# x^T from the host, the first norm folded into q, k, v and gate, transposed out-projections, in a two-layer decoder trunk

## The chip, the cores and the metric

The kernel runs on one core of one Trainium2 chip. The metric is device time in microseconds of one execution. Engines: PE (TensorE, matmuls and transposes), DVE (VectorE), ACT (ScalarE), POOL (GpSimd), SP (SyncE, here the queue that issues all DMAs).

## What is computed

x is 1024 x 1024 (1024 positions, model width 1024), float32. Layer A is differential attention with 8 heads, layer B stick-breaking attention with 16 heads of width 64, worked on in 8 pairs; both have a SiLU gate:

```python
h = rms(x, a_norm)                       # rms: x * rsqrt(mean(x*x) + 1e-6) * gain
q, k, v, g = split(h @ a_w_in)           # 1024 columns each
q, k = rope(rms(q, q_norm)), rope(rms(k, k_norm))     # norm over 64 columns
o = rms((softmax(q1 k1) - lam * softmax(q2 k2)) v, subln) * (1 - lambda_init)
x1 = x + (o * silu(g)) @ a_w_out
k, v = split(rms(x1, kv_norm) @ w_kv)
q, g = split(rms(x1, b_norm) @ b_w_in)
out = x1 + (stick_breaking(q, k, v) * silu(g)) @ b_w_out
```

All products keep more than one float32r matmul's precision: each operand is split into a high part h (rounded to float32r) and a low part l = value - h, and a product is three matmuls, h*h + h*l + l*h.

## The kernel before

Positions are worked on in two halves of 512 and blocks of 128; kc counts the 8 chunks of 128 of the model width. The normed input of a layer lies transposed as the pair (ah, al), [128 of a chunk, 8 chunks, 512 positions] for each half. Layer A's head h needs four projections: q and k together by rows (`qk_steps`, line 624: 8 row blocks, 256-wide matmuls with ah stationary and the weights moving), v and gate transposed (`proj_t`, line 233: 512-wide with the weights stationary). Layer B's k, v, q and gate all go through `proj_t`. `group` (line 211) writes the matmuls of one sum into a PSUM bank of the tag "proj" (2 banks) and cuts them into steps; `merge` (line 313) interleaves the steps of the next head's projections with the attention of the current one (`unit_s`, `unit_t`). `Jobs` loads the weights one job ahead. For the last head the fill is the out-projection.

`norm_rows` (line 125) norms one block of 128 positions: square with a row sum on ACT, `rstd_of` (line 112: Ln and Exp on ACT, one Newton step on DVE), scaling on DVE, 8 transposes by PE into PSUM, then h by ACT and l by DVE. It is called for the 8 blocks of x at the start (lines 718 to 729) and by `sink_a` (line 763) for the 8 blocks of x1. The gains of the norms are multiplied into the weights when these are split (`split_w` with gain, lines 158 to 165; `park`, line 178, which splits layer B's weights during layer A and writes them back to DRAM).

`OutProj` has the mixer output oT stationary (`lhs`, line 449) and the out-weights moving, 256 columns at a time (`parts`, line 452; c counts four column groups), or 512 for the last two chunks of the first two groups (`rest`, line 465). A sum is added into a tile of 128 positions x 1024 (`xs`, lines 457 and 469) that held the residual. `sink_a` or `sink_b` follows when a block has its last column group. The half f0 is projected beside the last head's second half, f1 after it: `pre1` takes the first six chunks of one or two column groups ahead, lines 543 and 544 the rest in the order 2, 3, 1, 0.

`v_rows` (line 303) evacuates v from PSUM by ACT, then transposes it back to rows; `silu` (line 237) evacuates the gate by DVE with a clamp at -80, and has Exp, Ln, Exp on ACT and a product on POOL, set late.

The order of instructions on each engine is fixed when the kernel is built: a planner takes the code's order as priority, moves `hp()` blocks ahead and `later()` blocks back, and places instructions by estimated durations; on the chip each engine runs its own queue strictly in that order. Tiles of one tag share a number of buffers (B, line 45), and a tile that finds none free waits.

## Time and profile before

| | us |
|---|---|
| median of three runs | 1450.12 |
| lowest, highest | 1446.09, 1452.68 |
| profiled execution | 1446.61 |
| its span, first to last instruction | 1444.8 |
| busy: PE, DVE, ACT, POOL | 1400.6, 1052.9, 907.9, 299.7 |

Times within the profile count from the start of the span. An engine's busy time is the time in which at least one of its instructions ran; matmuls overlap in the pipeline, so the length of one is more than its share of PE. PEclk is the granted TensorE clock as a share of full speed.

### The profile page before, as it was taken

Reading aid. Unit: us, or ns where it says so; the run is one execution under the profiler, and the core shown is the slowest. Engines: PE = TensorE matmul, PEld = TensorE weight load, DVE = VectorE, ACT = ScalarE, POOL = GpSimd, SP = SyncE. Lnnn points to the kernel's source line nnn. Section 1 sums busy time; section 2 is a strip of 40 time slices with the busy share of each in tenths; the row PEclk is TensorE's granted clock in tenths of the full one; section 3 lists DMA queues with packets and bytes.
Section 4 is the critical chain, followed back from the end, with each engine's and each line's share of the span. In section 5 each row is a group of like instructions: output and inputs, shape, how many; then the busy total and the mean of one; then the engine's idle time right before and its main releaser. Section 6 shows DMA issues by size and latency. Waiting matters only on the chain. (4 is left out here: it accounts for less than half of the span.)

```text
span 1444.8 us, 24738 instructions
## 1 busy us (share of the span) xinstructions
PE 1400.6 (97%) x8944; PEld 1179.3 (82%) x8944; DVE 1052.9 (73%) x2145; ACT 907.9 (63%) x1834; POOL 299.7 (21%) x545
## 2 busy tenths in 40 slices
PE   8999999999999999989999999999999999988899
PEld 8887878787878787879987777787788778777699
DVE  7577888787879787885514867787868777878851
ACT  7566766676767565544225776778777777777610
POOL 0111212121212113000001231322324132424200
PEclk9999999999999999999999999999999999998999
DMA  5246453645464645641522121131212121343524
GB/s 205 82 152 193 145 194 122 200 135 190 132 199 145 219 154 184 203 176 74 171 83 88 59 73 53 52 114 43 78 59 89 58 88 59 136 157 126 224 89 145
DMA packets 94603, 185.93 MB, mean 129 GB/s; under 512 B 8721, under 2 KB 43793, under 8 KB 93457
## 3 DMA queue, kind: packets, MB, share of 16 engines
q1 hardware_dynamic: 94480, 184.35, 38.1%
q8 instruction: 71, 1.16, 0.3%
q14 instruction: 52, 0.42, 0.1%
HBM read 119.31 MB, written 65.01 MB: 128 GB/s over the span
## 5 line engine op out<-in xcount | busy, mean ns | idle before, releaser
L223 PE MATMUL proj<-ah,w 128*128 128x512 f32 x768 | 309.2, 403 | 0.0
L225 PE MATMUL proj<-ah,w 128*128 128x512 f32 x768 | 308.9, 402 | 0.0
L224 PE MATMUL proj<-al,w 128*128 128x512 f32 x768 | 307.5, 400 | 0.0
L223 PE MATMUL proj<-w,ah 128*128 128x256 f32 x992 | 285.8, 288 | 6.6 <-DVE v L457 3.9
L224 PE MATMUL proj<-w,ah 128*128 128x256 f32 x992 | 281.8, 284 | 0.0
L225 PE MATMUL proj<-w,al 128*128 128x256 f32 x992 | 280.9, 283 | 0.0
L223 PEld LDWEIGHTS proj<-w,ah 128*128 128x128 f32 x992 | 187.7, 189 | 15.3 <-DVE v L457 4.9
L224 PEld LDWEIGHTS proj<-w,ah 128*128 128x128 f32 x992 | 187.7, 189 | 5.1 <-issue 4.5
L225 PEld LDWEIGHTS proj<-w,al 128*128 128x128 f32 x992 | 187.7, 189 | 1.7 <-issue 0.6
L225 PEld LDWEIGHTS proj<-ah,w 128*128 128x128 f32 x768 | 144.3, 188 | 37.6 <-issue 7.1
L223 PEld LDWEIGHTS proj<-ah,w 128*128 128x128 f32 x768 | 144.3, 188 | 36.8 <-issue 6.3
L224 PEld LDWEIGHTS proj<-al,w 128*128 128x128 f32 x768 | 144.4, 188 | 34.9 <-issue 5.1
L855 DVE TENSOR_TENSOR_SCAN u4k<-zl,u4k 128x768 f32<-128x768 f32 (+4 forms) x96 | 171.4, 1791 | 1.1
L300 DVE TENSOR_TENSOR tl<-tr,th 128x512 fp32r<-128x512 f32 (+1 forms) x240 | 145.1, 628 | 33.7 <-ACT th L299 33.0
L265 PE MATMUL sc<-kh,q 64*128 64x512 f32 (+2 forms) x768 | 156.6, 396 | 10.7 <-DVE small L655 7.5
L856 ACT ACTIVATE zl<-u4k 128x768 f32<-128x768 f32 (+4 forms) x96 | 81.4, 848 | 112.9 <-DVE u4k L855 98.8
L299 ACT ACTIVATE th<-tr 128x512 fp32r<-128x512 f32 (+1 forms) x240 | 125.2, 552 | 30.7 <-PE tr L293 22.5
L853 DVE SCALAR_TENSOR_TENSOR u4k<-zl,u4k 128x768 f32<-128x768 f32 (+4 forms) x96 | 95.9, 1008 | 58.5 <-ACT u4k L852 58.1
L843 POOL TENSOR_SCALAR_AFFINE_SELECT zl<-zl 128x128 f32<-128x128 f32 (+1 forms) x96 | 80.3, 845 | 278.3 <-ACT zl L841 278.1
L293 PE MATMUL tr<-ident,zl 128*128 128x128 f32 x864 | 130.7, 279 | 5.0 <-DVE tl L300 3.0
L265 PEld LDWEIGHTS sc<-kh,q 64*128 64x128 f32 x768 | 75.3, 185 | 58.7 <-issue 19.9
L664 ACT ACTIVATE zl<-zl,small 128x256 f32<-128x256 f32 (+7 forms) x128 | 98.1, 767 | 34.6 <-DVE small L655 18.7
(150 smaller groups left out, 2581.5 us busy)
## 6 DMA issues: line engine op xcount, KB each, us to landing
w<-w_kv SPq DMA_DIRECT2D x32, 512.0 KB, 5.2
w<-w_b SPq DMA_DIRECT2D x32, 512.0 KB, 5.2
w<-w_o SPq DMA_DIRECT2D x24, 512.0 KB, 4.7
raw<-in_w_kv_dram SPq DMA_DIRECT2D x32, 256.0 KB, 2.9
w_kv<-ph SPq DMA_DIRECT2D x32, 256.0 KB, 2.8
w_kv<-raw SPq DMA_DIRECT2D x32, 256.0 KB, 3.2
raw<-in_w_b_dram SPq DMA_DIRECT2D x32, 256.0 KB, 3.0
w_b<-ph SPq DMA_DIRECT2D x32, 256.0 KB, 3.0
```

Of the source, the lines that this page charges most:

```text
L223: pe.matmul(box["p"], lh, rh, start=(j == 0), stop=False)
L224: pe.matmul(box["p"], lh, rl, start=False, stop=False)
L225: pe.matmul(box["p"], ll, rh, start=False, stop=last)
L265: pe.matmul(pts[:, c, :wm], q[a][HI[c], rs_], k[b][HI[c], off:off + wm], start=(a + b == 0), stop=(a == 1))
L293: pe.transpose(pt[:, o:o + P], a[:, (2 * t + b) * P:(2 * t + b + 1) * P], ident)
L299: act.activation(th[:, skip:], pt[:, skip:], AF.Copy)
L300: dve.tensor_tensor(tl[:, skip:], pt[:, skip:], f32(th[:, skip:]), ALU.subtract)
L664: act.activation(p[c][:, :n], p[c][:, :n], AF.Exp, bias=b, scale=-1.0, accum_out=s[:, c:c + 1])
L843: pool.affine_select(t3[:, :, n - P:], t3[:, :, n - P:], [[0, len(cs)], [-1, P]], ALU.is_ge, -BIG, base=-1, channel_multiplier=1)
L853: dve.scalar_tensor_tensor(u, zc, 0.0, u, ALU.min, ALU.subtract)
L855: dve.tensor_tensor_scan(ur, t[:, 1:w2 + 1][:, ::-1], ur, 0.0, ALU.add, ALU.subtract)
L856: act.activation(zc, u, AF.Exp, scale=-1.0)
```

## The change

x comes from the host as x^T in 8 chunks, [8, 128, 1024], x1 is kept in the same form, and the output leaves transposed (the host turns it back). The first norm: with r the factor 1/rms of a position, x^T times the gain is split into (ah, al) without r. For q and k the factor cancels in their own norm, if its epsilon is divided by r squared (`eps_r`); v and gate, which come transposed, are multiplied by `rx`, r along the free axis in all partitions, when they leave PSUM. r comes from squares on ACT, added up on POOL over the chunks, and `rstd_cols`: one-column matmuls add over the partitions, `rstd_of` follows, then four diagonal matrices and four matmuls with ones bring r to all partitions. Both out-projections have the weights stationary and oT moving, 512 wide; the residual tiles hold two chunks x 512 positions, and a sum goes to the sink when its last chunk is added. `sink_a` collects the squares of a half's 8 pieces, and after the eighth calls `rstd_cols` and scales and splits all 8. The gains leave `split_w`. The clamp of layer A's gate moves to POOL, v's evacuation in layer A from ACT to DVE. The buffers change: g2k 2 in layer A, raw 4 instead of 3 (with `park`'s high parts, which had the tag ph with 2), small 8 instead of 9.

```diff
-    g2k = lambda: T("g2k", [P, HALF], B["g2k"])
+    g2k = lambda: T("g2k", [P, HALF], B["g2k" + "ab"[layer[1]]], pool=layer[0])
...
-    def rstd_of(ss, n, scale):
-        ln = small(n)
-        act.activation(ln, ss, AF.Ln, bias=eps, scale=scale)
+    def rstd_of(ss, n, scale, eps_r=None):
+        m = small(n)
+        if eps_r is None:
+            dve.tensor_scalar(m, ss, scale, EPS, ALU.mult, ALU.add)
+        else:
+            j = n // eps_r.shape[1]
+            dve.scalar_tensor_tensor(m.rearrange("p (k j) -> p k j", j=j), ss.rearrange("p (k j) -> p k j", j=j), scale,
+                                     eps_r.unsqueeze(2).to_broadcast([P, n // j, j]), ALU.mult, ALU.add)
         y = small(n)
...
+        act.activation(y, m, AF.Ln)
+        act.activation(y, y, AF.Exp, scale=-0.5)
...
-    def norm_rows(x, ah, al, r):
-        xn = zt()
-        ss = small(1)
-        act.activation(xn, x, AF.Square, accum_out=ss)
-        y = rstd_of(ss, 1, 1.0 / D)
-        dve.tensor_scalar(xn, x, y, None, ALU.mult)
-        for g in range(2):
-            t = PS("tr", B["tr"])
-            for j in range(4):
-                kc = g * 4 + j
-                pe.transpose(t[:, j * P:(j + 1) * P], xn[:, kc * P:(kc + 1) * P], ident)
-            t3 = t.rearrange("p (k c) -> p k c", k=4)
-            h = ah[:, g * 4:g * 4 + 4, r * P:(r + 1) * P]
-            l = al[:, g * 4:g * 4 + 4, r * P:(r + 1) * P]
-            act.activation(h, t3, AF.Copy)
-            dve.tensor_tensor(l, t3, f32(h), ALU.subtract)
+    def rstd_cols(acc, eps_r=None):
+        pm = PS("tr", B["tr"])[:, :4]
+        for r in range(4):
+            pe.matmul(pm[:, r:r + 1], acc[:, r * P:(r + 1) * P], ones[:, 0:1], start=True, stop=True)
+        ss = small(4)
+        dve.tensor_copy(ss, pm)
+        y = rstd_of(ss, 4, P / D)
+        if eps_r is not None:
+            dve.tensor_scalar(eps_r, ss, EPS * P / D, EPS * EPS, ALU.mult, ALU.add)
+        pb = PS("tr", B["tr"])
+        d = T("raw", [P, HALF], B["raw"], pool=layer[0])
+        for r in range(4):
+            dve.tensor_scalar(d[:, r * P:(r + 1) * P], ident, y[:, r:r + 1], float(P), ALU.mult, ALU.mult)
+        for r in range(4):
+            pe.matmul(pb[:, r * P:(r + 1) * P], ones, d[:, r * P:(r + 1) * P], start=True, stop=True)
+        return pb
+    def add_squares(acc, x, first):
+        sq = T("raw", [P, HALF], B["raw"], pool=layer[0])
+        act.activation(acc if first else sq, x, AF.Square)
+        if not first:
+            pool.tensor_tensor(acc, acc, sq, ALU.add)
...
-            h = T("ph", [P, HALF], B["ph"], F32R, pool=layer[0])
+            h = T("raw", [P, HALF], B["raw"], pool=layer[0]).bitcast(F32R)
...
-    def silu(pg, u):
+    def silu(pg, u, r=None):
         g = g2k()
         with hp():
-            dve.tensor_scalar(g, pg, -80.0, None, ALU.max)
+            if r is None:
+                dve.tensor_scalar(g, pg, -80.0, None, ALU.max)
+            else:
+                dve.tensor_tensor(g, pg, r, ALU.mult)
         with later():
+            if r is not None:
+                pool.tensor_scalar(g, g, -80.0, None, ALU.max)
...
-    def v_rows(pt):
+    def v_rows(pt, r=None):
         vt = g2k()
         with hp():
-            act.activation(vt, pt, AF.Copy)
+            if r is None:
+                act.activation(vt, pt, AF.Copy)
+            else:
+                dve.tensor_tensor(vt, pt, r, ALU.mult)
...
-                rb = hf * 4 + r
-                nc.sync.dma_start(t, self.xres[rb * P:(rb + 1) * P, :])
+                nc.sync.dma_start(t.rearrange("p (k n) -> p k n", k=2), self.xres[2 * r:2 * r + 2, :, hf * HALF:(hf + 1) * HALF]
+                                  .rearrange("k p n -> p k n"))
...
-        def lhs(self, hf, kc, r):
-            return tuple(t[:, kc, r * P:(r + 1) * P] for t in self.oT[hf])
-        def parts(self, hf, cs, ks, out=None):
-            def add(r, c, pt):
-                with hp():
-                    xs = self.xr[hf][r][:, c * 256:c * 256 + 256]
-                    dve.tensor_tensor(xs, pt, xs, ALU.add)
-                if out:
-                    self.sink(hf * 4 + r, self.xr[hf][r], out)
-            return lambda W: [st for r0 in (0, 2) for i, c in enumerate(cs) for r in (r0, r0 + 1) for st in
-                              group(256, [lambda kc=kc, r=r, i=i: (self.lhs(hf, kc, r), W["w"][i](kc)) for kc in ks],
-                                    lambda pt, r=r, c=c: add(r, c, pt))]
+        def add(self, hf, d, pt, final):
+            xs = self.xr[hf][d // 2][:, d % 2 * HALF:d % 2 * HALF + HALF]
+            with hp():
+                dve.tensor_tensor(xs, pt, xs, ALU.add)
+            if final:
+                self.sink(hf, d, xs)
+        def group(self, hf, d, ws, ks):
+            return group(HALF, [lambda kc=kc: (ws(kc), tuple(t[:, kc, :] for t in self.oT[hf])) for kc in ks],
+                         lambda pt: self.add(hf, d, pt, ks[-1] == KC - 1))
+        def parts(self, hf, cs, ks):
+            return lambda W: [st for i, c in enumerate(cs) for j in range(2) for st in self.group(
+                hf, 2 * c + j, lambda kc, i=i, j=j: tuple(t[:, j * P:(j + 1) * P] for t in W["w"][i](kc)), ks)]
         def rest(self, hf):
-            def add(r, pt):
-                with hp():
-                    xs = self.xr[hf][r][:, :HALF]
-                    dve.tensor_tensor(xs, pt, xs, ALU.add)
-            return lambda W: [st for r in range(4) for st in
-                              group(HALF, [lambda kc=kc, r=r: (self.lhs(hf, kc, r), W["w"][kc]) for kc in range(self.nk, KC)], lambda pt, r=r: add(r, pt))]
+            return lambda W: [st for d in range(4) for st in self.group(
+                hf, d, lambda kc, d=d: tuple(t[:, d * P:(d + 1) * P] for t in W["w"][kc]), range(self.nk, KC))]
...
-            y = rstd_of(ss[0], 16, 1.0 / 64)
+            y = rstd_of(ss[0], 16, 1.0 / 64, eps_r[hf])
...
+    def load_x(hf, i):
+        tag = ("v", "v", "v", "v", "kh", "kl", "kh", "kl")[hf * 4 + i]
+        xp[hf, i] = T(tag, [P, 2, HALF], 4 if tag == "v" else 2)
+        nc.sync.dma_start(xp[hf, i], x_t[2 * i:2 * i + 2, :, hf * HALF:(hf + 1) * HALF].rearrange("k p n -> p k n"))
+    def split_x(hf, i):
+        for j in range(2):
+            kc = 2 * i + j
+            h, l = (t[:, kc, :] for t in xT[hf])
+            act.activation(h, xp[hf, i][:, j], AF.Copy, scale=cols[:, kc:kc + 1])
+            dve.scalar_tensor_tensor(l, xp[hf, i][:, j], cols[:, kc:kc + 1], f32(h), ALU.mult, ALU.subtract)
+    def squares(hf):
+        acc = T("o", [P, HALF], B["o"])
+        for kc in range(KC):
+            add_squares(acc, xp[hf, kc // 2][:, kc % 2], kc == 0)
+        act.activation(rx[hf], rstd_cols(acc, eps_r[hf]), AF.Copy)
     nc.sync.dma_start(cols, ins["cols"])
-    norm_x(0)
-    w_first = [[w_mov(w_qk[0], cols[:, 0:8])]]
-    for rb in range(1, 4):
-        load_x(rb)
-        norm_x(rb)
-    w_first.append(w_pair(w_vg[0], cols[:, 0:8]))
+    load_x(0, 0)
+    w_first = [[w_mov(w_qk[0])]]
+    for i in range(1, 4):
+        load_x(0, i)
+    for i in range(4):
+        split_x(0, i)
+    squares(0)
+    w_first.append(w_pair(w_vg[0]))
     started.append(1)
-    for rb in range(4, 8):
-        load_x(rb)
-        norm_x(rb)
+    for i in range(4):
+        load_x(1, i)
+        split_x(1, i)
+    squares(1)
...
-    def sink_a(rb, t, cs):
-        nc.sync.dma_start(x1[rb * P:(rb + 1) * P, :], t)
-        if xT2[rb // 4] is None:
-            xT2[rb // 4] = (T("ah", [P, KC, HALF], 2, F32R), T("al", [P, KC, HALF], 2, F32R))
-        norm_rows(t, *xT2[rb // 4], rb % 4)
+    acc_a = [None, None]
+    def sink_a(hf, d, xs):
+        nc.sync.dma_start(x1[d, :, hf * HALF:(hf + 1) * HALF], xs)
+        if acc_a[hf] is None:
+            acc_a[hf] = [T("o", [P, HALF], B["o"]), []]
+        acc, pieces = acc_a[hf]
+        add_squares(acc, xs, not pieces)
+        pieces.append((d, xs))
+        if len(pieces) < KC:
+            return
+        xT2[hf] = (T("ah", [P, KC, HALF], 2, F32R), T("al", [P, KC, HALF], 2, F32R))
+        rb = rstd_cols(acc)
+        for d, xs in sorted(pieces, key=lambda e: e[0]):
+            h, l = (t[:, d, :] for t in xT2[hf])
+            dve.tensor_tensor(xs, xs, rb, ALU.mult)
+            act.activation(h, xs, AF.Copy)
+            dve.tensor_tensor(l, xs, f32(h), ALU.subtract)
...
-        "x": x[0],
+        "x": x[0].T.reshape(KC, P, S),
```

## Rows read from the trace of the kernel before

**Rows 1.** Busy time by stage: length, PE, PEld, DVE, ACT, POOL, clock, DMA, GB/s.
```profile
14.10:66.50 52.40, 52.15 (x353) 46.75 (x351) 36.49 (x106) 34.05 (x84) 6.03 (x9) 1.00 0.27 90
66.50:580.00 513.50, 505.62 (x3366) 426.30 (x3366) 408.99 (x1088) 335.48 (x785) 97.82 (x148) 1.00 0.52 170
580.00:735.00 155.00, 148.63 (x1113) 135.78 (x1113) 101.37 (x268) 66.33 (x146) 6.29 (x21) 0.99 0.43 147
735.00:1280.00 545.00, 541.25 (x2999) 429.78 (x2998) 397.65 (x506) 388.41 (x670) 156.29 (x295) 1.00 0.24 81
1280.00:1390.00 110.00, 91.50 (x637) 79.89 (x636) 89.35 (x126) 73.46 (x129) 31.38 (x62) 0.91 0.37 135
```

**Rows 2.** Costliest groups: busy us, mean ns of one, idle before.
```profile
L223 PE MATMUL proj<-ah,w 128*128 128x512 f32 x768 | 309.2, 403 | 0.0
L223 PE MATMUL proj<-w,ah 128*128 128x256 f32 x992 | 285.8, 288 | 6.6 <-DVE v L457 3.9
```

**Rows 3.** PE in order of time: start, length, instruction; mid layer A.
```profile
99.83 0.28 PE L223 MATMUL proj<-w,ah 128*128 128x256 f32 x1
...
100.54 0.39 PE L223 MATMUL proj<-ah,w 128*128 128x512 f32 x1
...
101.47 0.39 PE L224 MATMUL proj<-al,w 128*128 128x512 f32 x1
```

**Rows 4.** PE in order of time, where x1's transposes stand between projections.
```profile
722.59 0.39 PE L225 MATMUL proj<-ah,w 128*128 128x512 f32 x1
722.82 1.03 PE L136 MATMUL tr<-ident,zl 128*128 128x128 f32 x8
723.61 0.48 PE L223 MATMUL proj<-ah,w 128*128 128x512 f32 x1
723.93 0.60 PE L136 MATMUL tr<-ident,zl 128*128 128x128 f32 x4
```

**Rows 5.** Busy time of line 136 alone, in two stretches: PE, PEld.
```profile
0.00:45.00 45.00, 9.91 (x64) 8.46 (x64) 0.96 0.46 165
580.00:735.00 155.00, 8.77 (x64) 7.44 (x64) 0.99 0.43 147
```

**Rows 6.** Line 691: lengths, min/median/max ns; PE's wait for it, 580 to 735.
```profile
L691 PE MATMUL tr<-t1k,ones x64: 377/378/483, 89.8 to 665.5; 128*128 128x256 f32 x64
...
PE tr L691 <- ACT t1k L689: 0.5, 1, 0.5
```

**Rows 7.** DMA rate from 0 to 45 us in 40 slices; PE at the start.
```profile
GB/s 0 131 354 274 361 361 346 397 419 390 408 428 393 393 395 399 381 273 204 22 7 0 0 0 148 91 8 0 0 0 0 0 15 0 0 0 0 0 0 0
...
14.13 0.36 PE L225 MATMUL proj<-w,al 128*128 128x256 f32 x1
```

**Rows 8.** Prices of 512-wide operations on ACT, DVE and POOL.
```profile
L189 ACT ACTIVATE ph<-raw,cols 128x512 fp32r<-128x512 f32 x64 | 45.7, 720 | 63.5 <-DMA raw<-in_w_kv_dram 24.6 <-DMA raw<-in_w_b_dram 21.4 <-DMA w_kv<-ph 4.4
L190 DVE SCALAR_TENSOR_TENSOR raw<-raw,cols,ph 128x512 fp32r<-128x512 f32 x64 | 50.8, 800 | 27.6 <-ACT ph L189 27.1
...
L386 POOL TENSOR_TENSOR o<-o,o x28: 1272/1298/3329, 147.8 to 1328.9; 128x512 f32<-128x512 f32 x28
```

**Rows 9.** ACT and DVE in order of time: one block's norm.
```profile
712.09 0.29 ACT L114 ACTIVATE small<-small,eps 128x1 f32<-128x1 f32 x1
...
713.98 0.75 DVE L131 TENSOR_SCALAR zl<-v,small 128x1024 f32<-128x1024 f32 x1
```

**Rows 10.** In order of time: weights split on DVE, and PE's first use.
```profile
349.35 1.67 DVE L165 SCALAR_TENSOR_TENSOR w<-raw,cols,w 128x256 fp32r<-128x256 f32 x4
...
395.65 0.40 PE L223 MATMUL proj<-ah,w 128*128 128x512 f32 x1
```

**Rows 11.** Residual adds: the last one, a 512-wide form; PE's wait, 1270 to 1400.
```profile
1441.73 0.42 DVE L457 TENSOR_TENSOR zl<-proj,zl 128x256 f32<-128x256 f32 x1 [2.40 <-PE proj L225]
...
L469 DVE TENSOR_TENSOR kh<-proj,kh x2: 680/685/690, 641.7 to 1370.5; 128x512 f32<-128x512 f32 x2
...
PE proj L223 <- DVE v L457: 4.8, 2, 3.8
```

More of the change, by code (lines that the diff above doesn't have):

```diff
@@ L151, in split_w @@
             raw = T("raw", [P, HALF], B["raw"], pool=layer[0]) if started else T("o", [P, HALF], B["o"])
-            r3 = raw.rearrange("p (k n) -> p k n", k=k)
+            r3 = raw.rearrange("p (k n) -> p k n", k=h.shape[1])
             nc.sync.dma_start(raw if len(src.shape) == 2 else raw.rearrange("p (k n) -> p k n", k=src.shape[1]), src)
-            if gain is None:
-                act.activation(h, r3, AF.Copy)
-                dve.tensor_tensor(l, r3, f32(h), ALU.subtract)
-                return
@@ L158, in split_w @@
-            for i in range(k):
-                r, g = r3[:, i], gain[:, i:i + 1]
-                n_w[0] += 1
-                if n_w[0] <= B["wp"]:
-                    dve.tensor_scalar(h[:, i], r, g, None, ALU.mult)
-                else:
-                    act.activation(h[:, i], r, AF.Copy, scale=g)
-                dve.scalar_tensor_tensor(l[:, i], r, g, f32(h[:, i]), ALU.mult, ALU.subtract)
+            act.activation(h, r3, AF.Copy)
+            dve.tensor_tensor(l, r3, f32(h), ALU.subtract)
```

69 lines of the change are left out of this document (29 added, 40 removed).

## The prediction

> **What bounds the kernel now.** I read the busy time by stage first, because a share over the whole span would mix stages with different limits. In [rows 1] the kernel is cut at the points where its work changes: up to 66.5 us head 0 of layer A is projected, to 580 the other heads run, to 735 layer A's out-projection and the norm behind it, to 1280 layer B's heads, to 1390 its last head, then out-projection alone. The reader is to see that PE is busy 52.15 of 52.40, 505.62 of 513.50, 148.63 of 155.00 and 541.25 of 545.00 us, at a granted clock of 0.99 to 1.00, with DVE at 80% or less. Whatever PE no longer has to do in these stages comes off the end. Two places differ: the first 14 us, in which PE waits for x and its norm, and 1280 to 1390, where PE idles 18.5 us, the clock falls to 0.91 and DVE is busy 89.35 of 110: there a chain through DVE sets the pace.
>
> The second view is matmuls in order of time, since a duration says little for pipelined work. A 256-wide matmul starts 0.118 us after the one before it (six from 99.83 to 100.54), a 512-wide one after 0.2325 us (four from 100.54 to 101.47) [rows 3].
>
> **The change, part by part.** The times before are 1446.1 to 1452.7; the profiled execution took 1446.6 (span 1444.8, so 1.8 lies around it), 3.5 below the median of 1450.1. The sum is made against it.
>
> *Transposes of x (removed).* `norm_rows` issued 128 of them, 64 at the start and 64 between the layers [rows 5]. Eight take 0.79 us of PE (722.82 to 723.61), and the matmul behind them gives way 0.32 instead of 0.2325 us later [rows 4], so eight cost 0.88 us and 64 cost 7.0. The upper bound is their busy time, 9.9 and 8.8 us, which counts overlap twice.
>
> *Out-projection turned.* The weights become the stationary operand, the mixer output the moving one, 512 wide. Of 992x3 = 2976 256-wide matmuls [rows 2], 8 heads x 8 row blocks x 8 kc x 3 = 1536 are the q/k projection and stay; the other 1440 become 720 512-wide ones. By [rows 3]: 1440 x 0.118 = 169.9 against 720 x 0.2325 = 167.4 us; rounding in the rows makes this -1 to -2.5, and I take -1.2. Halving the count brings almost nothing: PE already streams without a gap for weight loads.
>
> *The new norm's sums.* `rstd_cols` runs four times (two halves of each norm), each with 4 one-column and 4 128-column f32 matmuls. Such a matmul is two instructions: the 32 calls of line 691 stand as x64 [rows 6]. So a call has 16. The nearest rows are the 128-column transposes, also f32 and in fours to eights, at 0.10 to 0.11 us apart [rows 4]: 1.75 us a call. The other end is no overlap at all, 16 x 0.378 [rows 6] = 6.0; no group of like matmuls in the trace behaves so. I take 1.75, four times 7.0.
>
> *The start.* Now the steady stream begins at 14.1 us [rows 7]: PE needs the first norm before its first projection. After, it needs x^T of half 0 (2 MB) and the first weights (1 MB), and no norm. Adding the GB/s slices of 1.125 us, 3.15 MB have come by about 10.6 us [rows 7]. The last piece then takes two splits on ACT and one on DVE behind them, 0.72 + 0.72 + 0.80 = 2.2 us [rows 8]: about 13. But two row groups hold the two PSUM banks meanwhile and can do 6 of their 8 kc, 36 matmuls or 4.2 us, in the gaps between pieces. The stream starts as if at 8.9, 5.2 earlier. Within the stream, 48 of the 64 transposes go (-5.3; 16 stood ahead of 14.1) and two calls come (+3.5): -7.0. What hides the rest is ACT: 16 splits, 16 squares and 8 weight splits at no more than 0.72 are 28.8 us from 4 on, so 33, and half 1 is wanted at 8.9 + 22.4 + 3 = 34. With that cover so thin I charge 1.0: **-6.0**; ends -9 and 0.
>
> *Between the layers.* 64 transposes go and two calls come: -7.0 + 3.5 = **-3.5**. What is late next: half 1's norm can start only when its last column group is summed, then come add, square and POOL add (0.69 + 0.72 + 1.30 [rows 8, 11]), the sums (0.9, half a call), the chain from Ln to the scaled row (1.9 us, 712.09 to 713.98 [rows 9]), the diagonals (about 1, an estimate from the 0.75 us of 1024 columns in [rows 9] and three more starts) and the broadcast (0.9), 7.4 us in all, and then 8 x (0.69 + 0.80) = 12 us on DVE. The cover is layer B's head 0 on half 0, four projections of 24 x 0.2325 = 22.4 us. 19.4 is under 22.4, so nothing is charged; where the cover is gone, rival 1 has the price.
>
> *Waits for PSUM banks.* 256-wide sums of six matmuls lasted 0.7 us against an add of 0.42 (1441.73); afterwards they last 1.4 against 0.69 [rows 11]. Between 1270 and 1400 PE waited 4.8 us for such an add. I take -1.5; ends -5 and, since the fill between attention steps is cut anew in the stage where DVE sets the pace, +8.
>
> *The tail.* The last add is 512 wide, 0.69 instead of 0.42, and its store twice as large: +0.4.
>
> *Costed at nothing.* v's scaling moves from ACT to DVE with its priority kept, while the weights' gain leaves both engines (half as many instructions over the same columns); the gate's clamp goes to POOL, idle over 80% of its time in layer A's heads [rows 1], one operation of about 1.3 us ahead of ACT's three, which are wanted a head later. The q/k norm's Ln now waits for a DVE operation; its result is wanted a job (some 40 us) later. `park` takes two of four `raw` slots where it had slots of its own, and weight loads queue with it on SP; but the weights split up to 351 are first used at 395.65 [rows 10], 44 us of cover. x1 goes out as 16 stores for 8 on SP, nothing behind them is due at once.
>
> Sum: -6.0 - 3.5 - 1.2 - 1.5 + 0.4 = -11.8. From the profiled execution that is 1434.8, from the median 1438.3; I forecast **1437**.
>
> Two rules of the Trainium skill were weighed. In the trace eight transposes need 0.79 us [rows 4]. "TensorE: Matmul & The Clock Gate", Part 4: PE-mode transpose, gives some 275 ns for one in a kernel's context; as time on PE that would make the 128 worth 35 us, but the rows show that figure only as the length of one, overlapped by the next. POOL's adds of this size last 1.30 us in the median and up to 3.33 [rows 8]. "SBUF — State Buffer", Who interferes with whom, says that a DVE instruction with two SBUF inputs and a POOL instruction that reads SBUF lock each other out whole; the 14 new POOL adds at the start meet 16 DVE splits with two SBUF inputs, so by that rule the end 0 of the start would be near.
>
> **Rivals.**
> 1. *PE stands in its queue at the new sums: slower.* The order on PE is fixed when the kernel is built. If `rstd_cols`'s matmuls lie ahead of work that is ready, PE waits once for the square and POOL add (2.0 to 4.1 us by [rows 8]) and once for the chain to the diagonals (1.9 + 1): 5 to 7 a call, 20 to 28 for four, 1437 + 24 = 1461. It makes the kernel slower than 1450 from 3.3 us a call. For it: POOL is in this chain, 7 adds in a row at the start, 9 us. Against: line 691 has the same shape (square, matmul, Ln) 32 times, and from 580 to 735 PE waited 0.5 us for it in all [rows 6], because other matmuls had been put between. All four calls: 7%. Two of them, 1449: 10%.
> 2. *The DVE-paced stage of layer B falls otherwise.* The same work, cut into other pieces; PE idles 18.5 us there now. Half of that more or less is +8 or -8: 1445 or 1429. For it: it is the one stage where the order decides. Against: nothing in it grows, and DVE's adds shrink. 8% for the worse, 6% for the better.
> 3. *The full gain.* The start at -9, bank waits at -5, that stage unhurt: 1437 - 3 - 3.5 = 1430.5, and with less of the sums' matmuls than 1.75 a call and that stage in luck 1425. 15%.
> 4. *Transposes cost their whole length.* 128 x 0.286 us would be 36.6 instead of 14.0, giving 1414. The eight in 0.79 us speak against it. 1%.
> 5. *The change buys nothing:* the time taken from PE returns as idle time in the same stages, 1446 to 1452. It would need another engine at its limit; DVE at 80% in layer A is the nearest [rows 1]. 5%.
>
> **How the numbers follow.** The forecast, 1430 to 1443, has 48%. About 0.5%, 7.3 us, is what a measurement of this kernel can tell from no change: faster means under 1442.9, slower over 1457.4. Faster: forecast 48, full gain 15, the better side of rival 2 6, transposes 1: 70%. Slower: rival 1 in full, 7%. The rest, 10 + 8 + 5 = 23%, is no change. The range reaches from the full gain to the two half-lost cases, 1425 to 1450, leaving out some 8% below and 12% above.
>
> **What would show it.** Right: the 256-wide out-projection groups gone, 512-wide ones 0.23 us apart; head 0's stage ends near 60 us instead of 66.5; no PE wait of over 1 us for the sums; layer B's first K done while half 1 is still being split; PE's total near 8 us lower. Wrong: PE idle ahead of the one-column matmuls, ACT's squares ahead of the last splits of half 0, a PE gap where layer B's half 1 begins, or idle time from 1270 to 1380 that differs by more than 8 us.

## The result, and the profile after

The changed kernel took **1458.4 us** (median of 9 runs, 1454.7 to 1463.0) against 1447.3 (1445.0 to 1452.7) for the kernel before on the same chip: ratio 1.0071, 95% interval 1.0052 to 1.0089. It is slower by 0.7%, where 1437 was forecast, 1425 to 1450 the range. The profiled execution took 1456.3, with a span of 1454.5, 9.7 more than before's.

By stage, cut as in [rows 1] (length, PE, PEld, DVE, ACT, POOL, clock, DMA, GB/s):

```profile
14.10:66.50 52.40, 47.72 (x298) 42.77 (x299) 38.45 (x82) 28.49 (x64) 23.65 (x22) 0.97 0.29 95
66.50:580.00 513.50, 504.47 (x3341) 427.70 (x3340) 397.10 (x1040) 313.72 (x714) 119.26 (x161) 1.00 0.53 167
580.00:735.00 155.00, 136.70 (x685) 108.39 (x684) 97.47 (x222) 63.86 (x131) 26.73 (x29) 0.96 0.43 146
735.00:1280.00 545.00, 538.89 (x2973) 429.58 (x2971) 397.12 (x513) 380.80 (x658) 153.60 (x299) 1.00 0.22 73
1280.00:1390.00 110.00, 96.87 (x530) 75.15 (x529) 90.99 (x119) 79.41 (x139) 28.45 (x63) 0.91 0.56 199
```

The prediction set out from the sentence that whatever PE no longer has to do comes off the end. PE does have less to do: its busy time fell from 1400.6 to 1393.4 us, near the 8 forecast, although more of it ran at half clock. But PE now idles 4.7 us at the start for 0.25, and 18.3 us from 580 to 735 for 6.4 [rows 1]. Over all these stages idle time grew by 14.5 us. And some of the idle time costs a second time, because the clock falls behind it, as shown below: the mean granted clock went from 0.990 to 0.985, which over the spans is 14.4 us of lost full speed before and 21.8 after.

A cut at fixed times compares different work. So I also counted the columns of the projections' matmuls (both kernels stream the same number) in order of time, and took the times at which shares of them had started. A tenth is the work of two of layer A's heads: about four tenths are layer A's heads, the next tenth its out-projection, the next four layer B's heads, the last tenth its out-projection. This table, worked out from the traces, serves for all runs. The stretches are those of one execution, and the last one ends where the last of these matmuls starts, some 4 us before the end of the span. L is `leadb`, explained below. The median is that of all executions of a kernel; the kernels ran on several chips, and the ratio is to the kernel before on the same chip:

```
kernel, profiled run          0-10%  10-40%  40-50%  50-90%  90-100%   median   ratio
before                        128.8   448.4   139.4   558.5    166.3   1447.3   1
before, L .03 (e11)           129.6   449.2   140.4   562.8    157.5   1444.6   0.9975
before, L .01 (e15)           130.3   449.0   139.5   574.0    149.4   1447.1   0.9992
after                         131.8   448.3   153.5   558.9    157.8   1458.4   1.0071
after, L .03 (e13)            130.9   444.2   152.5   561.2    160.2   1460.8   1.0076
after, L .01 (e14)            131.5   445.3   153.1   574.3    150.9   1461.0   1.0086
e1 adds on DVE                130.2   448.5   156.0   555.8    162.5   1456.4   1.0062
e2 start alone                131.2   448.5   142.8   554.4    167.4   1446.0   0.9993
e3 out-projection alone       131.6   450.5   152.1   563.2    160.4   1462.6   1.0103
e4 norm out of raw            131.7   444.5   148.4   559.0    153.2   1442.8   0.9967
e10 = e4, L .03               131.6   447.8   148.2   561.5    160.8   1454.1   1.0035
e5 = e4 + e1                  131.2   448.7   147.2   555.7    162.6   1448.1   0.9999
e6 = e3, norm out of raw      132.9   449.9   141.9   562.6    160.0   1453.4   1.0028
e7 stores on ACT              131.5   445.7   153.5   559.2    153.1   1450.4   1.0020
e8 = e4, products on POOL     131.5   449.0   149.3   558.9    159.8   1452.6   1.0024
e9 = e4, first sums on PE     131.7   445.2   144.4   557.7    153.5   1438.5   0.9930
e16 = e9, L .03               131.5   445.6   146.2   560.1    160.3   1450.3   1.0008
e12 = e4, no row scale        130.7   446.8   139.9   560.8    154.1   1434.3   0.9900
e17 = e4, park through o      130.7   447.0   145.0   557.5    158.8   1443.6   0.9962
e18 = e9, park through o      128.4   446.8   151.0   559.2    159.7   1451.0   1.0019
```

After against before: +3.0 in the first tenth (forecast -6), **+14.1 from four to five tenths** (layer A's last head and out-projection with the second norm; forecast some -4), and -8.1 from half to the end, in layer B (forecast about -2).

**The first tenth.** Line 726 makes the low part of a piece of x^T on DVE (count, min/median/max ns, first and last start):

```profile
L726 DVE SCALAR_TENSOR_TENSOR al<-v,cols,ah x8: 740/1768/1773, 6.6 to 19.3; 128x512 fp32r<-128x512 f32 x8
L726 DVE SCALAR_TENSOR_TENSOR al<-kh,cols,ah x4: 735/740/742, 22.6 to 26.0; 128x512 fp32r<-128x512 f32 x4
...
  PE proj L227: 4.1, 6
```

The eight of the first half, beside POOL's additions of squares, take 1.77 us in the median, those of the second half 0.74; PE waits for them six times, 4.1 us. The stream that was to be complete at 13 us is so at 21, and from 24.3 on 256-wide matmuls start 0.214 us apart (24.33 to 25.83, seven intervals) where [rows 3] show 0.118: the lower of the clock's two levels.

**From four to five tenths.** That stretch by itself (columns as above), before and after:

```profile
577.20:716.70 139.50, 133.13 (x1044) 123.35 (x1044) 96.27 (x257) 60.77 (x134) 5.96 (x13) 0.99 0.44 151
580.10:733.60 153.50, 135.20 (x677) 107.15 (x677) 96.68 (x219) 63.72 (x130) 26.73 (x29) 0.96 0.43 145
```

PE idles 6.4 us of it before and 18.3 after, and the granted clock falls from 0.99 to 0.96. So most of the 14 us is waiting, and a part is the clock. PE's waits from 560 to 740 us (total, times, longest):

```profile
PE proj L225 <- DVE kh L462: 5.2, 2, 3.2
PE proj L225 <- ACT w L166: 3.9, 3, 2.6
PE av L689 <- ACT th L306: 3.0, 1, 3.0
```

The longest of the waits of SP's queue from 640 to 720 us:

```profile
SPq L784 <- DVE kh L462: 41.7, 4, 24.1
```

And that queue in order of time (start, length):

```profile
663.15 15.82 SPq L784 DMA_DIRECT2D x<-qk  x3
703.20 2.12 SPq L784 DMA_DIRECT2D x<-kh  x2
705.41 2.25 SPq L165 DMA_DIRECT2D raw<-in_a_w_out_dram  x4
```

Three different things are late here. Weights of the out-projection are issued only at 705 us and, the last four, at 713, behind a store of x1 (line 784) that waits 24 us for its sum. DVE, in order of time, has the eight products of the second norm (line 796) ahead of the sum at 702.49 (line 462), for which PE waits 3.2 us, and eight more operations of that norm (line 798) around the next sums:

```profile
697.70 1.29 DVE L796 TENSOR_TENSOR kh<-kh,tr 128x512 f32<-128x512 f32 x2 [0.66 <-PE tr L146]
...
702.49 0.68 DVE L462 TENSOR_TENSOR kh<-proj,kh 128x512 f32<-128x512 f32 x1
...
706.10 3.57 DVE L798 TENSOR_TENSOR al<-qk,ah 128x512 fp32r<-128x512 f32 x4
709.60 1.27 DVE L462 TENSOR_TENSOR kl<-proj,kl 128x512 f32<-128x512 f32 x2
```

And ACT, in order of time, stands from 591 us at a weight split (line 166) whose load is not in, with the attention's casts (line 306) queued behind:

```profile
590.84 0.58 ACT L306 ACTIVATE th<-tr 128x512 fp32r<-128x512 f32 x1
596.03 0.63 ACT L166 ACTIVATE w<-raw 128x512 fp32r<-128x512 f32 x1 [4.61 <-DMA raw<-in_a_w_out_dram]
596.57 0.96 ACT L306 ACTIVATE th<-tr 128x512 fp32r<-128x512 f32 x2
```

Behind these waits the clock falls: the windows from 596 to 604 and 700 to 714 us (columns as above) show 0.79 and 0.76.

```profile
596.00:604.00 8.00, 5.75 (x33) 4.70 (x33) 4.76 (x15) 6.37 (x16) 0.00 (x0) 0.79 0.91 297
700.00:714.00 14.00, 8.18 (x21) 6.20 (x22) 13.28 (x21) 8.23 (x14) 3.21 (x2) 0.76 0.43 151
```

### The profile page after: what moved, and what is told of

The parts are those of the page before. It is cut to its first block, busy times and chain, and to the rows that moved or that the text cites. A ratio compares the mean times of both kernels' runs of the same rounds, so it can differ in the third digit from the quotient of the medians.

```text
span 1454.5 us, 22998 instructions
## 1 busy us (share of the span) xinstructions
PE 1393.4 (96%) x8160; PEld 1141.2 (78%) x8160; DVE 1049.0 (72%) x2015; ACT 883.7 (61%) x1734; POOL 357.7 (25%) x589
## 4 chain that ended last, share of the span: by engine, by line
PE 71%; DVE 11%; DMA 7%; ACT 6%; issue 4%; POOL 1%; SPq 0%; ACTq 0%; POOLq 0%; DVEq 0%
PE proj L225 16%; PE proj L226 16%; PE proj L227 16%; PE sc L272 7%; PE tr L300 5%; DVE u4k L886 2%; PE av L903 2%; PE av L902 2%; DVE tl L307 1%; PE av L689 1%; DMA raw<-in_b_w_out_dram 1%; PE av L691 1%; PE av L690 1%; DMA raw<-in_w_kv_dram 1%; ACT u4k L882 1%
## 5 line engine op out<-in xcount | busy, mean ns | idle before, releaser
L225 PE MATMUL proj<-ah,w 128*128 128x512 f32 x1008 | 404.6, 402 | 9.1 <-ACT w L166 3.9
L226 PE MATMUL proj<-al,w 128*128 128x512 f32 x1008 | 404.2, 401 | 0.0
L227 PE MATMUL proj<-ah,w 128*128 128x512 f32 x1008 | 400.0, 397 | 0.2 <-DVE w L167 0.2
L225 PEld LDWEIGHTS proj<-ah,w 128*128 128x128 f32 x1008 | 190.9, 189 | 56.9 <-issue 8.1
L226 PEld LDWEIGHTS proj<-al,w 128*128 128x128 f32 x1008 | 190.8, 189 | 43.0 <-issue 6.7
L227 PEld LDWEIGHTS proj<-ah,w 128*128 128x128 f32 x1008 | 190.5, 189 | 42.5 <-issue 5.0
L272 PE MATMUL sc<-kh,q 64*128 64x512 f32 (+2 forms) x768 | 156.0, 398 | 8.8 <-ACT zl L872 5.1
L225 PE MATMUL proj<-w,ah 128*128 128x256 f32 x512 | 149.7, 293 | 4.9 <-DVE g2k L246 4.3
L227 PE MATMUL proj<-w,al 128*128 128x256 f32 x512 | 147.9, 290 | 4.1 <-DVE al L726 4.1
L226 PE MATMUL proj<-w,ah 128*128 128x256 f32 x512 | 147.9, 289 | 0.9 <-DVE w L167 0.9
L874 POOL TENSOR_SCALAR_AFFINE_SELECT zl<-zl 128x128 f32<-128x128 f32 (+1 forms) x96 | 70.8, 745 | 293.4 <-ACT zl L872 293.0
L300 PEld LDWEIGHTS tr<-ident,zl 128*128 128x128 f32 x864 | 101.4, 142 | 21.8 <-ACT zl L887 6.2
L225 PEld LDWEIGHTS proj<-w,ah 128*128 128x128 f32 x512 | 98.4, 192 | 11.1 <-DVE g2k L246 5.3
L227 PEld LDWEIGHTS proj<-w,al 128*128 128x128 f32 x512 | 98.3, 192 | 8.3 <-DVE al L726 5.3
```

Source lines behind the costliest of these rows:

```text
L225: pe.matmul(box["p"], lh, rh, start=(j == 0), stop=False)
L226: pe.matmul(box["p"], lh, rl, start=False, stop=False)
L227: pe.matmul(box["p"], ll, rh, start=False, stop=last)
L272: pe.matmul(pts[:, c, :wm], q[a][HI[c], rs_], k[b][HI[c], off:off + wm], start=(a + b == 0), stop=(a == 1))
L300: pe.transpose(pt[:, o:o + P], a[:, (2 * t + b) * P:(2 * t + b + 1) * P], ident)
L874: pool.affine_select(t3[:, :, n - P:], t3[:, :, n - P:], [[0, len(cs)], [-1, P]], ALU.is_ge, -BIG, base=-1, channel_multiplier=1)
```

## The experiments

**Which half of the change costs?** Two kernels have one half each: e2 the new start and the folded norm with the old out-projections, e3 the turned out-projections and the new second norm with the old start.

```diff
 # e2: OutProj, sink_a, sink_b, norm_rows of the kernel before; x given in both layouts
 # e3: load_x, norm_x, w_mov(gain), v_rows, silu, park of the kernel before; x given in both layouts
```


> The kernel before with the new start alone: x^T from the host for the first norm (x by rows as well, for the residual), the norm folded into q, k, v and gate, the buffers of the changed kernel; the out-projections and the norm between the layers as before. If the loss lies in the out-projection and the norm between the layers, this one stands at 1447 plus or minus 3, since in the changed kernel head 0's stage ended only 3 us late. If the folding (v on DVE, the clamp on POOL, two g2k buffers, shared raw buffers) costs along layer A, it stands at 1452 or more. The prediction's step for the start would have 1441.

> The kernel before with the turned out-projections and the half-wise norm between the layers alone: x by rows for the first norm as before, x^T as well for the residual, the buffers of the kernel before. If the loss lies between the layers, the stage from 580 us on loses 8 to 14 us here too, layer B's last head gives some 8 back, and the time is 1450 to 1457. The prediction's steps for these parts would have 1441 to 1443.

e2: 1446.0, ratio 0.9993 (0.9980 to 1.0006). e3: 1462.6, ratio 1.0103 (1.0088 to 1.0118), more than the 1457 expected at most. The loss comes with the out-projection and second norm; the start neither gains the 6 us forecast nor loses any that the end shows. From four to five tenths PE idles 5.8 us in e2, about as long as in the kernel before, and 18.6 in e3.

**POOL's additions.**

```diff
-            pool.tensor_tensor(acc, acc, sq, ALU.add)
+            dve.tensor_tensor(acc, acc, sq, ALU.add)
```


> The changed kernel with the squares added up on DVE instead of POOL (one word in add_squares), nothing else. Theory A: POOL's adds and DVE's splits of x, both with two inputs in SBUF, shut each other out, and that paced the first stream of projections (a split took 1.77 us beside POOL's adds, 0.74 without). Then every split takes 0.74 to 0.80, the last sum of half 0 is reached near 17 us instead of 21, and the time falls by 3 to 6 us from 1458, to 1452 to 1455. Rival B: the splits are slow for another reason (waits for ACT or for the DMAs); then a split stays above 1.2 us and the time stays within 2 us of 1458 or rises with DVE's 28 extra operations.

1456.4, ratio 1.0062 (1.0047 to 1.0077). The splits came down as expected, to

```profile
L726 DVE SCALAR_TENSOR_TENSOR al<-v,cols,ah x8: 743/746/752, 6.3 to 16.7; 128x512 fp32r<-128x512 f32 x8
```

so the 1.77 was the price of meeting POOL's additions. This is the rule of the Trainium skill ("SBUF — State Buffer", Who interferes with whom) that the prediction weighed, and the trace agrees with it: 1768 ns beside them, 746 without. But the time fell by 2 us only, which is less than expected and not clear of noise: DVE now does the additions itself, 0.69 each, and PE, which waited 4.1 us for the splits, now waits 1.2 us for them and 2.6 for the additions.

**Raw slots or SP's queue?** The second norm's squares and diagonals lie in `raw` tiles, of which there are four and into which weights are loaded; and x1's stores stand in SP's queue ahead of those loads. e4 moves the temporaries, e7 the stores.

```diff
 # e4: in sink_a's add_squares, and in rstd_cols where eps_r is None
-        sq = T("raw", [P, HALF], B["raw"], pool=layer[0])
-        d = T("raw", [P, HALF], B["raw"], pool=layer[0])
+        sq = g2k()
+        d = g2k()
 # e7: in sink_a, behind add_squares
-        nc.sync.dma_start(x1[d, :, hf * HALF:(hf + 1) * HALF], xs)
+        act.dma_start(x1[d, :, hf * HALF:(hf + 1) * HALF], xs)
```


> The changed kernel with the squares and the diagonals of the norm between the layers taken from the two g2k buffers, which are idle by then, instead of from the four raw buffers that the out-projection's weights need too. Theory C: weights that find no raw buffer, and stand in SP's queue behind stores of x1, made PE wait for them (2.6 us at 710 us, with the clock halved after). Then the loads of the last weights are issued 15 us or more ahead of their use, the wait for them is gone, and the time is 3 to 7 us under 1458. Rival: the wait comes from the adds that stand behind 16 operations of the norm on DVE (3.2 us at 703 us); then the time stays within 2 us of 1458.

> The changed kernel with the raw slots as they are and only the stores of x1 moved: issued from ScalarE behind the square that reads the same tile, not from SyncE ahead of the weight loads. If the weights came late because a store on SyncE's queue waited for a sum (41.7 us in four waits), most of the 15.7 us comes back: 1443 to 1447 us, weights issued near 680 us. If they came late because squares held the raw slots: 1456 to 1459 us, with the weight loads still issued near 700 us and waiting for a raw slot. A split of the two gives between.

e4: 1442.8, ratio 0.9967 (0.9954 to 0.9980). e7: 1450.4, ratio 1.0020 (1.0006 to 1.0033). SP's queue in e4, in order of time:

```profile
680.41 11.97 SPq L165 DMA_DIRECT2D raw<-in_a_w_out_dram  x4
693.25 5.71 SPq L784 DMA_DIRECT2D x<-kh  x2
```

The longest waits of SP's queue in e7, 640 to 720 us:

```profile
SPq L165 <- POOL o L154: 33.8, 6, 15.7
```

In e4 the last weights go out from 680 us on, 25 us sooner and ahead of the stores, and PE's wait for line 166 is gone; the stretch falls from 153.5 to 148.4. In e7 no store is left on SP, and the loads wait all the same, 33.8 us, for POOL's additions to give the squares' slots back; its stretch is 153.5, as after, and PE idles 19.2 us in it. So it is the slots that hold the loads. The queue that caught my eye first, with its 24 us, was a consequence. (In e7 PE waits only 0.6 us for the weights themselves; its longest wait after 700 us, 2.0 us, is for a sum that stands on DVE behind the split of a late weight.)

Neither total is explained by this stretch alone. e4 came out 15.6 us lower than the changed kernel, where 3 to 7 were expected, and only 5.1 of that lie here; 4.6 lie in the last tenth and 3.8 between one and four tenths, where the two kernels have the same order. e7's total lies between the two expected; what it gained lies in those two stretches too. The runs on the order below size this. The stretch of e4 by itself shows what the slots gave:

```profile
576.10:724.50 148.40, 136.97 (x678) 109.86 (x677) 96.18 (x219) 62.89 (x130) 26.54 (x29) 0.92 0.45 150
```

PE idles 11.4 us for 18.3, but at a clock of 0.92 for 0.96 (0.94 in e10 below, which has the same order there). e6 repeats the test without the new start:

```diff
 # e6 = e3 + e4
```


> The kernel before with the turned out-projections and the half-wise second norm alone (1462.6 us so far), now with that norm's squares and diagonals out of the weights' raw slots. If the turned out-projection lost its time because squares and late stores kept the next weights out, it comes down by some 16 us, to 1443 to 1448 us, and the loss at 710 us falls from 17 us to 8 or less. If the loss is in the turning itself (512-wide sums, adds behind the norm on VectorE), it stays above 1456 us.

1453.4, ratio 1.0028 (1.0016 to 1.0040): the stretch falls from 152.1 to 141.9, more than the total's 9 us, and PE idles 9.3 us in it for 18.6; the total lies between the two expected. The largest wait that went, 7.2 us at 653 us in e3, is one for the attention (`zl`, line 690) and not for a weight, so part of these 10 us is the order that came out with the slots.

**Do the two repairs add, and is DVE's order the rest?** e5 has e4 and e1; e8 takes the eight products of the second norm off DVE:

```diff
 # e8 = e4 +
-        rb = rstd_cols(acc)
+        rb = T("o", [P, HALF], B["o"])
+        act.activation(rb, rstd_cols(acc), AF.Copy)
-            dve.tensor_tensor(xs, xs, rb, ALU.mult)
+            pool.tensor_tensor(xs, xs, rb, ALU.mult)
```


> The changed kernel with both edits tried singly before: the second norm's squares and diagonals from the two-kilobyte pool instead of the weights' raw slots (alone 1442.8 us), and all sums of squares added on VectorE instead of GpSimd (alone 1456.4 against 1458.4 us). If the two losses are separate terms: 1440 to 1441.5 us, with the first-half splits of L726 at 0.74 us and the weights issued near 680 us as before. If what each gives is mainly a new order of the plan: anything between 1438 and 1452.

> The kernel with the second norm's temporaries out of the raw slots (1442.8 us), and in it the eight products x1 times rstd of each half on GpSimd, from a copy in SBUF, so that VectorE has eight operations fewer ahead of the sums of the out-projection. If the 4.8 us that TensorE waits there for a sum are the price of the order on VectorE: 1438 to 1441 us, loss at 710 us 3 to 5 us instead of 8. If GpSimd's eight additions of 1.3 us and their contention with VectorE's splits set the end of the norm instead: 1444 to 1452 us.

e5: 1448.1, ratio 0.9999 (0.9990 to 1.0009). e8: 1452.6, ratio 1.0024 (1.0011 to 1.0036). Neither came out as separate terms: against e4 the stretch is hardly moved, 147.2 and 149.3. (Against e1, which has the shared slots, e5's stretch is 8.8 us shorter, and PE idles 12.8 us in it for 20.0: a third pair for the slots.) But e5's last tenth takes 162.6 us and e4's 153.2, with the same instructions there. So the next question was the order.

**How much does the order alone move?** `leadb` is one number by which `merge` weaves fill work into layer B's heads. With 0.03 or 0.01 for 0.02 the instructions stay the same, in another order from some 770 us on in the changed kernel and its variants, and from some 865 us on in the kernel before.

```diff
-"leadb": 0.02
+"leadb": 0.03        # e14, e15: 0.01
```


> The kernel of 1442.8 us with one number of the hand-written order changed (the lead of fill work in layer B's heads 0.03 for 0.02): the same instructions in another order from 740 us on. It sizes how far the order alone moves the last head. If the last head's gain over the kernel before (13.1 us here, 8.5 in the changed kernel, 3.7 with the adds on VectorE) is a matter of the edits: within 2 us of 1442.8. If it is a matter of the order that happens to come out: 1443 to 1453 us, with the stretch from nine tenths of the projections to the end at 153 to 163 us.

> The kernel before with the same one number changed (0.03 for 0.02). If the order alone moves the last head, its stretch from nine tenths of the projections to the end differs from 166.3 us by several us, up or down, and the time lies between 1440 and 1455 us; if before's last head is set by its own work, it stays at 166 to 168 us and the time within 2 us of 1448.

> The changed kernel with the lead of fill work in layer B's heads 0.03 for 0.02: another order from 740 us on, nothing else. Up to then it must stand where the changed kernel stands (some 17 us behind the kernel before at half of the projections). If the loss is the edits' and the order averages out: 1452 to 1465 us. If the changed kernel's 1458 is a bad draw of the order: below 1450.

> As the run before it, with 0.01 for 0.02: a third order of the changed kernel. If the loss is the edits': 1452 to 1465 us, the stretch from nine tenths of the projections to the end between 153 and 163 us. If a bad draw: below 1450.

> The kernel before with 0.01 for 0.02: its third order (0.03 gave 1444.6 us, 0.02 some 1448). Expected 1443 to 1452 us, so that the mean of its orders stays under that of the changed kernel's by 8 us or more if the loss is the edits', and by less than 4 us if it is the order's.

e10: 1454.1, ratio 1.0035 (1.0023 to 1.0047), 0.68% or some 10 us above e4. The window from 1280 to 1390 us in e4:

```profile
1280.00:1390.00 110.00, 101.66 (x558) 78.74 (x555) 90.88 (x121) 75.16 (x132) 24.59 (x59) 0.97 0.51 175
```

and in e10:

```profile
1280.00:1390.00 110.00, 93.42 (x503) 73.55 (x502) 84.51 (x113) 74.16 (x128) 23.18 (x59) 0.88 0.53 181
```

PE idles 8.3 us there in the one and 16.6 in the other, at 0.97 and 0.88 of the clock, and gets through 558 matmuls in the one and 503 in the other. The kernel before moves less: 0.9975 (0.9956 to 0.9994) and 0.9992 (0.9975 to 1.0008). The changed kernel stays where it was: 1.0076 (1.0048 to 1.0105) and 1.0086 (1.0063 to 1.0109). So the loss is not this order's: the means of three orders are 0.9989 and 1.0078. The stretch from four to five tenths, 139.4 to 140.4 against 152.5 to 153.5, lies ahead of what `leadb` moves; these are repetitions of one order, and show that the stretch repeats to 1 us. Between one and four tenths the same repetitions differ by 4 us (444.2 to 448.3), so a difference of that size there, in one profile, says nothing. The order inside the stretch from four to five tenths was not varied by itself; what speaks for the slots is that all three pairs with and without shared slots, each with another order, move the same way. Layer B from half to the end takes 724.8, 720.3 and 723.4 us before, 716.7, 721.4 and 725.2 after: 1.7 less in the mean, so most of the 8.1 us gained there in the first profile was the order.

**The start without additions.** In e9 TensorE adds the first half's squares itself, in PSUM, with 32 products of four columns.

```diff
 # e9 = e4 +, in squares(0): pick[:, 5 * r] is 1 / P, the rest 0
+                for r in range(4):
+                    pe.matmul(pm[:, :4], sq[:, r * P:(r + 1) * P], pick[:, 4 * r:4 * r + 4],
+                              start=kc == 0 and r == 0, stop=kc == KC - 1 and r == 3)
```


> The kernel of 1442.8 us, and in it the squares of the first half of x are no longer added on GpSimd: TensorE adds them in PSUM, 32 products of four columns, in the stretch in which it waits for the splits. If the late start (+3 us at a tenth of the projections) comes from VectorE's splits being locked out by GpSimd's additions: L726 at 0.74 us throughout, the first stream complete some 4 us sooner, time 1437 to 1440 us. If TensorE's own 32 products (3.5 us) and the clock at half speed at 24 us take that back: 1442 to 1445 us.

> The kernel of 1438.5 us (temporaries out of the raw slots, first squares summed by TensorE) with 0.03 for 0.02. If its gain over the kernel before is the edits': 1436 to 1446 us. If it is mostly the order that came out, as 1442.8 against 1454.1 us for the kernel without TensorE's sums says: 1446 to 1452 us.

e9: 1438.5, ratio 0.9930 (0.9906 to 0.9953), the lowest of the kernels that compute the whole. The splits did come down, to 0.75 us, and the first stream is complete at 16.5 us instead of 21. Yet the gain is not there: head 0's stage of e9,

```profile
14.10:66.50 52.40, 52.40 (x329) 48.99 (x329) 33.09 (x80) 28.18 (x64) 15.50 (x16) 0.90 0.31 101
```

shows PE never idle, but at a clock of 0.90, which is 5.2 us of the 52.4; the first tenth takes 131.7 us as in e4. The gain came in the stretch from four to five tenths, whose order is another than e4's: PE idles there as long as in e4, 11.9 against 11.4 us, at a clock of 0.96 instead of 0.92. e16, the same kernel with `leadb` 0.03, gave 1450.3, ratio 1.0008 (0.9993 to 1.0024). Two orders of it average 0.9969, two of e4 1.0001, so that "faster than before" is a statement on e9's order as much as on its edits.

**The rest of the stretch.** e12 leaves out the scaling of v and gate, which also puts v's evacuation back on ACT and the gate's clamp back on DVE; e17 and e18 give a parked weight's high part an `o` tile, so that `park` holds one raw slot and not two.

```diff
 # e12 = e4 +
-            tr = v_rows(pt, rx[hf])
+            tr = v_rows(pt)
-              ... heads_a, sink_a), (0, 1), extra, rx)
+              ... heads_a, sink_a), (0, 1), extra)
 # e17 = e4 +, e18 = e9 +
-            h = T("raw", [P, HALF], B["raw"], pool=layer[0]).bitcast(F32R)
+            h = T("o", [P, HALF], B["o"]).bitcast(F32R)
```


> The kernel of 1442.8 us without the multiplication of v and gate by rstd (v copied by ScalarE, gate bounded by VectorE, as before): that scaling is left out of the computation, rstd itself is still made. If these operations on VectorE and GpSimd are what is left of the loss at layer A's last head and out-projection (8.9 us there, 2.5 us in the kernel with the old start): that stretch loses 3 to 5 us less and the time is 1437 to 1441 us. If the loss there belongs to the turned out-projection: the stretch stays within 1.5 us and the time at 1441 to 1445 us.

> The kernel of 1442.8 us (norm's temporaries out of the raw slots), and in it the high part that a parked weight goes out from lies in one of the six o tiles, so that parking holds one raw slot at a time and not two. If parking is what makes the weights of the out-projection late near 590 us (ScalarE waits 4.1 us for such a load with the attention's casts behind it, TensorE waits 3.2 us for them and then runs at half clock): that wait goes, the stretch from four to five tenths of the projections falls from 148.4 to 141 to 145 us, and the time to 1436 to 1441 us, or 1447 to 1451 with an order in layer B like that of 1454.1. If the o tiles become the late thing instead, or the scaling of v and gate is the cause by its own work: the stretch stays at 147 us or more.

> The kernel of 1438.5 us (the first half's squares summed by TensorE) with the same move of the parked high part. Its stretch from four to five tenths is 144.4 us already. If parking costs there too: 140 to 142 us and 1434 to 1438 us in all. If not, within 2 us of 1438.5, or up to 1450 us where layer B's order comes out as in the slower variants.

e12: 1434.3, ratio 0.9900 (0.9877 to 0.9924), more than expected; its stretch is 139.9, nearly before's own length. The window from 575 to 612 us in e4:

```profile
575.00:612.00 37.00, 33.31 (x175) 26.15 (x174) 28.89 (x69) 22.70 (x47) 3.93 (x4) 0.91 0.63 199
```

in e12:

```profile
575.00:612.00 37.00, 37.00 (x210) 29.45 (x209) 32.17 (x74) 22.45 (x48) 2.00 (x5) 1.00 0.71 228
```

and in e17:

```profile
575.00:612.00 37.00, 31.01 (x158) 23.47 (x157) 29.19 (x71) 21.24 (x45) 9.54 (x10) 0.91 0.75 244
```

Without the scaling PE does not idle there at all, and the clock stays up. But over the whole stretch of e12,

```profile
577.50:717.40 139.90, 129.23 (x661) 102.33 (x660) 93.08 (x211) 58.52 (x123) 23.93 (x26) 0.99 0.45 152
```

PE idles 10.7 us, nearly as in e4 (11.4), at a clock of 0.99 instead of 0.92: most of what went with the scaling is clock. And e2, which has the scaling and the parking in raw slots beside the old out-projection, is only 3.4 us longer than before in this stretch; the scaling costs what it does only together with the turned out-projection and the new norm. e17: 1443.6, ratio 0.9962 (0.9949 to 0.9974), the time of e4 and not the lower one expected; the stretch falls to 145.0, but PE idles 11.9 us in it, and ScalarE's wait is replaced by others (a wait of 2.6 us for the cast remains). e18: 1451.0, ratio 1.0019 (1.0001 to 1.0037); the stretch rises to 151.0, where 140 to 142 was expected. So parking's second slot is not shown to be a cause; that the `o` tiles have a price of their own is a guess from e18. Whether the scaling costs by its own time on DVE and POOL, by the place that it gives ScalarE's weight splits, or by the order that comes out with it, stays open.

## Why the prediction was wrong, point by point

- **Prices of PE's work: right.** The sums' matmuls were sized well. Their groups on PE (busy us, mean ns, idle before):

```profile
L135 PE MATMUL tr<-ones,o 128*128 128x1 f32 x32 | 3.9, 243 | 0.6 <-POOL o L154 0.6
L146 PE MATMUL tr<-raw,ones 128*128 128x128 f32 x32 | 4.7, 281 | 1.0 <-DVE raw L144 1.0
```

  8.6 us with overlap counted twice, against 7.0 charged. PE waited 1.6 us for them in all, so rival 1 did not happen in the place it named.
- **Waits for PSUM banks: right in sign.** From 1270 to 1400 us PE waited 6.0 us for a sum before and 0.2 after, where 1.5 had been taken off.
- **The start: failed.** "Two splits on ACT and one on DVE behind them", each at the durations of [rows 8], was worked out with every engine alone. DVE's took 1.77 us beside POOL, and the end 0 of the range was still too kind: head 0's stage, forecast to end near 60 us instead of 66.5, ended 3 us later than before in the first profiles (2 us in the mean of three each). A second missing term is the clock: from 14.1 to 66.5 us it is 0.97 in the changed kernel and 0.90 in e9, 1.00 before [rows 1]. PE's first projection started 4 us sooner, and nothing of that was left at the end of the stage.
- **"Costed at nothing": the step that failed, by most of the 14 us.** "44 us of cover" was said of parking, "nothing behind them is due at once" of x1's stores. Each looked at one resource at a time; the stores did stand ahead of weights that were due, but e7 shows that they were not what cost. Nowhere in the working do the second norm's squares take raw slots, though the diff has it in `add_squares` and `rstd_cols`. Four raw slots served parking, squares, diagonals and the out-projection's weights in the same 100 us (in e3, three slots and a part of the parking elsewhere). Taking the norm's out took some 7 us of idle time off PE and gave 5 us of that stretch here (153.5 to 148.4), 9 with the squares added on DVE (156.0 to 147.2) and 10 in the kernel with the old start (152.1 to 141.9). A further 8.5 went with the scaling of v and gate (148.4 to 139.9, e12), which stood in the same list with its "priority kept", most of it as clock. The terms cost together: with the old out-projection (e2) the scaling and the parking cost 3.4 us there. Why the scaling costs more beside the turned one stays open.
- **Between the layers, -3.5: not seen.** Where this part was charged nothing, it held: layer B's head 0 covered the second half's norm, and PE has no wait from 733 to 800 us. But the first half's norm was not looked at: its eight products on DVE stand ahead of a sum that PE waits for, 3.2 us after and 2.8 in e4. e8 moved them to POOL and the stretch did not fall.
- **The clock: missing as a term.** The windows above show it fall behind the waits that end at 597, 703 and 710 us. From 0.990 to 0.985 is 7.4 us over the span, as much as the whole saving in PE's busy time.
- **Rival 2 and the range.** Layer B did come out otherwise, to the better and by the 8 us given; but over three orders that is 1.7, so this was luck, and it hid a part of the loss. The chance of slower, 7%, stood on one mechanism in one place. It should have counted that several edits were "costed at nothing" in one stage, in which PE was busy 148.63 of 155.00 us [rows 1].

## What to carry to other kernels

List every tile that an edit allocates, by the pool and tag that it takes, and find who else needs that tag in the same stretch: a slot shared with weight loads is a wait on the loads. A term costed at nothing is worth nothing only if all of its covers hold together; and where the trace has half-clock stretches behind waits, a new wait is to be charged with one. Before a gain of under 1% is believed, change one number of the order that leaves the work as it is: here that alone moved one kernel by some 10 us.

## What the runs showed of the hardware

A DVE split with two SBUF inputs went from 0.74 to 1.77 us beside POOL additions, and these took 1.61 us in the median there, where the fastest took 1.28. And PE busy without a gap was granted less than the full clock. From 14.1 to 34 us, before and in e9:

```profile
14.10:34.00 19.90, 19.65 (x150) 18.47 (x149) 18.27 (x65) 17.53 (x48) 0.00 (x0) 1.00 0.41 142
14.10:34.00 19.90, 19.90 (x122) 19.52 (x122) 15.41 (x37) 15.25 (x32) 3.38 (x3) 0.74 0.33 121
```

In e9 (second line, columns as above) it is 19.90 of 19.90 us busy at 0.74, where the kernel before had 1.00. What PE did ahead of the fall was projections with groups of e9's four-column products between; what it did in the kernel before was projections and transposes. Why the clock fell is not shown.
